# A two-layer decoder trunk in which the first feed-forward product becomes seven 2x2 block products

## The chip, the core and the metric

The kernel runs on one core of one Trainium2 chip, in one launch. The metric is the device time of a run in microseconds (us). Profiles and traces are of one execution each.

## What is computed

A decoder trunk of two layers over 1024 tokens of width 1024, all in f32. In each layer a modulation vector (`silu(c) @ W_ada + b`) gives shifts, scales and gates. A first half mixes differential attention and a gated convolution branch. The change is in the second half:

```python
x = x + (1.0 + gate1) * mixed
h2 = rms_norm(x, norm2_g[l]) * (1.0 + scale2) + shift2
f_gate, f_up = jnp.split(h2 @ w_ffn_in[l], 2, axis=-1)
x = x + (1.0 + gate2) * ((jax.nn.silu(f_gate) * f_up) @ w_ffn_out[l])
```

`w_ffn_in` is 1024 x 5632 (22 gate tiles and 22 up tiles of 128 columns), `w_ffn_out` is 2816 x 1024.

## The kernel before, in words

Activations lie transposed: 128 features on the partitions, tokens along the free axis, in two halves of 512 tokens (`HF`); `xs[j]` is feature tile j of the residual. Every f32 matrix operand is split into a high and a low float32r part, and a product is three matmuls per 128-feature tile: high x high, high x low, low x high. `wslab` (L131) loads a weight slab with a DMA on SyncE's queue (SP), rounds it to the high part on ScalarE (ACT, L139) and subtracts on GpSimd (POOL, L140) for the low part; `linear_half` (L143) then issues the three matmuls per feature tile for one token half (L148, L149, L152), each over 512 columns.

After the branch stage, the output projection runs for token half 0 and then half 1 (L745 to L757): eight output tiles of 24 matmuls (`pwo`), a residual update on VectorE (DVE, L753), squares on ACT and their sum on DVE (`sum_sq`), then `rstd_bcast` (a matmul over partitions, a power on POOL, four diagonal blocks L302, four matmuls L307) and `norm_half` (L317), which writes the split normalised activations.

In the feed-forward part, `ffn_in` (L770) makes hidden tile f: 24 matmuls for the gate tile and 24 for the up tile in each token half, a sigmoid on ACT (L784), two products on DVE that read PSUM (L785, L791), and the split of the result (ACT L792, POOL L793) in SBUF. `ffn_out` (L800) multiplies two or three hidden tiles with `w_ffn_out` and adds into `xs` (L812), so that the second product follows the first in `CHUNKS` of hidden tiles and nothing of it leaves SBUF. In layer 0, 48 modulation columns of layer 1 are made on the side (`ada_col`, L182: a load, a product on POOL at L188, a sum on ACT at L189, and one-column DVE operations at L192 to L199).

The program text is not the order of execution. The kernel is traced under a planner (`schedule_with_timeline_sim=True`, L909), which gives each engine and each DMA queue an order, with a place in the text as priority, and gives buffers out of pools; a pool that opens after another closed can use the same memory, and waits tile by tile. Engines then work through their queues in that order.

## Time and profile before

| | us |
|---|---|
| three runs, median (lowest to highest) | 3072.28 (3071.28 to 3072.49) |
| span of the profiled execution | 3069.9 |
| PE busy in it | 2876.6 (94%) |
| DVE, POOL, ACT busy | 1649.2, 1461.1, 1032.7 |

The profiled execution is 2.4 us under the median of the runs: its span goes from the first to the last instruction, and the rest of a run lies around it. Busy shares are means over stages with different limits, so the stages are read one by one.

### The profile page before, as it was taken

Reading aid. Unit: us, or ns where it says so; the run is one execution under the profiler, and the core shown is the slowest. Engines: PE = TensorE matmul, PEld = TensorE weight load, DVE = VectorE, ACT = ScalarE, POOL = GpSimd, SP = SyncE. Lnnn points to the kernel's source line nnn. Section 1 sums busy time; section 2 is a strip of 40 time slices with the busy share of each in tenths; the row PEclk is TensorE's granted clock in tenths of the full one; section 3 lists DMA queues with packets and bytes.
Section 4 is the critical chain, followed back from the end, with each engine's and each line's share of the span. In section 5 each row is a group of like instructions: output and inputs, shape, how many; then the busy total and the mean of one; then the engine's idle time right before and its main releaser. Section 6 shows DMA issues by size and latency. Waiting matters only on the chain.

```text
span 3069.9 us, 34308 instructions
## 1 busy us (share of the span) xinstructions
PE 2876.6 (94%) x13072; PEld 2366.5 (77%) x13072; DVE 1649.2 (54%) x2588; ACT 1032.7 (34%) x1820; POOL 1461.1 (48%) x974
## 2 busy tenths in 40 slices
PE   3788889999989999999999788999999999999998
PEld 3666768887768888888878677788888888888886
DVE  8899997644866211221278999774545211222126
ACT  4235445444444111111142455544534111111112
POOL 6856674435888332223342676554355232323323
PEclk9999999999989999999999999999999999999998
DMA  7611211245545111111142111222442111111113
GB/s 271 218 62 59 69 35 69 90 161 190 170 163 171 50 42 52 52 48 49 45 148 82 46 52 56 73 73 86 175 151 96 46 44 50 52 50 48 42 50 109
DMA packets 108502, 275.99 MB, mean 90 GB/s; under 512 B 10736, under 2 KB 38768, under 8 KB 108336
## 3 DMA queue, kind: packets, MB, share of 16 engines
q1 hardware_dynamic: 108336, 273.79, 25.9%
q8 instruction: 103, 1.69, 0.2%
q14 instruction: 63, 0.52, 0.1%
HBM read 235.90 MB, written 37.85 MB: 89 GB/s over the span
## 4 chain that ended last, share of the span: by engine, by line
PE 66%; DVE 24%; POOL 4%; DMA 2%; issue 2%; ACT 2%; POOLq 0%; SPq 0%; DVEq 0%; ACTq 0%
DVE uc L585 11%; PE pfg L149 5%; PE pfu L149 5%; PE pfg L152 5%; PE pfu L152 5%; PE pfg L148 5%; PE pfu L148 5%; PE pfo L148 5%; PE pfo L152 5%; PE pfo L149 5%; PE pg L152 2%; PE pg L148 2%; PE pg L149 2%; PE py L149 2%; PE py L152 2%
## 5 line engine op out<-in xcount | busy, mean ns | idle before, releaser
L140 POOL TENSOR_TENSOR wl<-wraw,wh 128x1024 fp32r<-128x1024 f32 (+2 forms) x296 | 672.5, 2274 | 1021.4 <-ACT wh L139 571.0
L139 ACT CAST wh<-wraw 128x1024 fp32r<-128x1024 f32 (+2 forms) x296 | 288.2, 974 | 732.8 <-PE pfo L149 353.2
L585 DVE SCALAR_TENSOR_TENSOR uc<-uc,vec 128x512 f32<-128x512 f32 x360 | 379.0, 1053 | 5.6
L812 DVE SCALAR_TENSOR_TENSOR x<-pfo,gcol,x 128x512 f32<-128x512 f32 x256 | 191.0, 749 | 265.0 <-PE pfo L152 264.9
L149 PE MATMUL pfg<-gl,wh 128*128 128x512 f32 x704 | 277.0, 393 | 4.7 <-DVE gl L329 3.6
L148 PE MATMUL pfo<-gh,wh 128*128 128x512 f32 x704 | 275.3, 391 | 4.1 <-DVE x L812 3.5
L148 PE MATMUL pfg<-gh,wh 128*128 128x512 f32 x704 | 276.3, 392 | 0.0
L148 PE MATMUL pfu<-gh,wh 128*128 128x512 f32 x704 | 275.3, 391 | 0.0
L149 PE MATMUL pfu<-gl,wh 128*128 128x512 f32 x704 | 275.2, 391 | 0.0
L149 PE MATMUL pfo<-gl,wh 128*128 128x512 f32 x704 | 274.8, 390 | 0.0
L149 PE MATMUL pg<-hl,wh 128*128 128x512 f32 x640 | 254.6, 400 | 14.3 <-DVE hl L511 14.3
L148 PE MATMUL pg<-hh,wh 128*128 128x512 f32 x640 | 254.0, 401 | 9.6 <-ACT hh L510 8.9
L785 DVE TENSOR_TENSOR fsg<-pfg,fsg 128x512 f32<-128x512 f32 x88 | 60.8, 691 | 375.5 <-ACT fsg L784 372.0
L791 DVE TENSOR_TENSOR fsg<-pfu,fsg 128x512 f32<-128x512 f32 x88 | 60.8, 691 | 328.0 <-PE pfu L152 327.9
L152 PE MATMUL pfo<-gh,wl 128*128 128x512 f32 x704 | 201.4, 391 | 0.0
L581 POOL TENSOR_TENSOR uc<-uc,ct 128x512 f32<-128x512 f32 x120 | 167.3, 1394 | 70.0 <-ACT ct L580 69.3
L793 POOL TENSOR_TENSOR gl<-fsg,gh 128x512 fp32r<-128x512 f32 x88 | 115.5, 1313 | 168.9 <-ACT gh L792 168.0
L152 PE MATMUL pg<-hh,wl 128*128 128x512 f32 x640 | 174.8, 403 | 0.0
L152 PE MATMUL pfu<-gh,wl 128*128 128x512 f32 x704 | 174.1, 390 | 0.0
L152 PE MATMUL pfg<-gh,wl 128*128 128x512 f32 x704 | 173.9, 390 | 0.0
L420 ACT ACTIVATE e<-psc,nb 128x512 f32<-128x512 f32 (+2 forms) x192 | 110.1, 578 | 169.1 <-DVE nb L417 148.9
L149 PEld LDWEIGHTS pfg<-gl,wh 128*128 128x128 f32 x704 | 133.4, 189 | 34.8 <-DVE gl L329 7.4
(228 smaller groups left out, 6143.1 us busy)
## 6 DMA issues: line engine op xcount, KB each, us to landing
wraw<-in_w_ffn_in_dram SPq DMA_DIRECT2D x100, 512.0 KB
adraw<-in_ada_w_dram SPq DMA_DIRECT2D x96, 512.0 KB
wraw<-in_w_in_dram SPq DMA_DIRECT2D x72, 512.0 KB
wraw<-in_w_ffn_out_dram SPq DMA_DIRECT2D x48, 384.0 KB
gd<-graw SPq DMA_DIRECT2D x64, 256.0 KB
gin<-gd SPq DMA_DIRECT2D x32, 512.0 KB
wraw<-in_w_out_dram SPq DMA_DIRECT2D x32, 512.0 KB
x<-in_xT_dram SPq DMA_DIRECT2D x16, 512.0 KB
```

Of the source, the lines that this page charges most:

```text
L139: S.copy(wh, raw)
L140: G.tensor_tensor(wl, raw, wh.bitcast(F32), op=ALU.subtract)
L148: PE.matmul(ps, wh[:, wc], rhs(0, k, hf), start=(k == 0), stop=False)
L149: PE.matmul(ps, wh[:, wc], rhs(1, k, hf), start=False, stop=False)
L152: PE.matmul(ps, wl[:, wc], rhs(0, k, hf), start=False, stop=(k == nk - 1))
L420: S.activation(e[:, n0:n1], pss[b][:, 0:n1 - n0], AF.Exp, bias=nb, scale=0.125, accum_out=sx[:, 2 * b + c:2 * b + c + 1])
L581: G.tensor_tensor(acc, acc, t, op=ALU.add)
L585: E.scalar_tensor_tensor(acc, u[:, k:k + HF], w, acc, op0=ALU.mult, op1=ALU.add)
L785: V.tensor_tensor(sgs[hf], ps, sgs[hf], op=ALU.mult)
L791: V.tensor_tensor(sgs[hf], ps, sgs[hf], op=ALU.mult)
L793: G.tensor_tensor(gl[:, hs], sgs[hf], gh[:, hs].bitcast(F32), op=ALU.subtract)
L812: V.scalar_tensor_tensor(xs[j][:, hs], ps, g2[:, j:j + 1], xs[j][:, hs], op0=ALU.mult, op1=ALU.add)
```

## The change

The first feed-forward product is done by `Group` for a pair of weight tiles (gate f, up f) as a 2x2 block product: two halves of the 1024 input features by two output tiles, times two feature halves by two token halves. Seven products `product(p)` of 12 matmuls each take the place of eight (96 matmuls). The operands of the weight side are sums made on DVE (`operand`), those of the activation side (`MV[1]` to `MV[7]`) are made once per layer, and the outputs are put together by `take1` to `take7` from PSUM. The gated product goes to a DRAM tensor `gf`; the residual after the output projection goes to `xm`. When all 22 groups are done, the second product runs by itself: for each token half, blocks of `gf` are loaded and split (`gblock`), and each of eight output tiles is one accumulation over all 22 hidden tiles, with `w_ffn_out` loaded and split once per token half. Modulation columns of layer 1 are made on DVE (`ada_col` without its last argument) beside groups 2 to 17. The convolution buffers and the rotary tables move into a pool of each layer, and the split activations are kept in units of four feature tiles. Cut to its core (comments that go, and `ffn_in` and `ffn_out`, which go whole, are left out):

```diff
-CHUNKS = [3, 3, 3, 3, 3, 3, 2, 2]
...
+    def rope_load(pl):
+        d3 = rope["d"]
+        Ct = rope["C"] = pl.tile([P, T], F32, name="Ct")
+        St = rope["S"] = pl.tile([P, T], F32, name="St")
...
+    def hunit(name, pl=None, tag="H", bufs=8):
+        return (pl or hp).tile([P, 4, HF], F32R, tag=tag, name=name, bufs=bufs)
+    class Parts:
+        def __init__(self, units):
+            self.units = units
+        def at(self, j):
+            return self.units[j // 4][:, j % 4, :]
     def hparts(name):
-        return [hp.tile([P, KT, HF], F32R, tag="H", name=f"{name}{p}", bufs=4) for p in "hl"]
+        return [Parts([hunit(f"{name}{p}{u}") for u in range(2)]) for p in "hl"]
...
+    xm = dr.tile([KT, P, T], F32, name="xm")
+    gf = dr.tile([FT, P, T], F32, name="gf")
...
+        csk = ExitStack()
+        cvp = csk.enter_context(pool("conv", side="right"))
+        rope_load(cvp)
...
+        fst = ExitStack()
+        H2 = fst.enter_context(pool("hextra"))
+        F = fst.enter_context(pool("ffn"))
+        def h2unit(name):
+            return hunit(name, H2, "H2", 6)
+        def split_into(hi, lo, src, E):
+            S.copy(hi, src)
+            E.tensor_tensor(lo, src, hi.bitcast(F32), op=ALU.subtract)
+        HS = [slice(hf * HF, hf * HF + HF) for hf in range(2)]
+        MV = {}
         for hf in range(2):
-            hs = slice(hf * HF, hf * HF + HF)
+            hs = HS[hf]
             Sq = nt("Sq")
             for j in range(KT):
                 ps = psct("pwo")
...
                 V.scalar_tensor_tensor(xs[j][:, hs], ps, gcol[l][0][:, j:j + 1], xs[j][:, hs],
                                        op0=ALU.mult, op1=ALU.add)
                 sum_sq(Sq, xs, hf, j)
+                DQ.dma_start(xm[j][:, hs], xs[j][:, hs])
             pb = rstd_bcast(Sq, 1.0 / D, 1e-6, "prn")
...
+            for q in range(2):
+                p = (1, 2, None, 3)[hf * 2 + q]
+                if p:
+                    un = h2unit if hf == 0 else hunit
+                    MV[p] = [un(f"b{p}{n}") for n in "hl"]
+                for jj in range(4):
+                    j = q * 4 + jj
+                    t = nt("ntt")
+                    V.scalar_tensor_tensor(t, xs[j][:, hs], acol[l][1][:, j:j + 1], pb, op0=ALU.mult, op1=ALU.mult)
+                    S.activation(xs[j][:, hs], t, AF.Identity, bias=modb[l][:, 24 + j:25 + j])
+                    if p:
+                        split_into(MV[p][0][:, jj, :], MV[p][1][:, jj, :], xs[j][:, hs],
+                                   V if hf and jj % 2 else G)
+        for jj in range(4):
+            a11, a12 = (xs[jj][:, h] for h in HS)
+            a21, a22 = (xs[4 + jj][:, h] for h in HS)
+            V.tensor_tensor(a11, a12, a11, op=ALU.subtract)
+            V.tensor_tensor(a12, a22, a12, op=ALU.subtract)
+            V.tensor_tensor(a22, a22, a11, op=ALU.subtract)
+        for p, x0, h in ((6, 4, 1), (7, 0, 1), (5, 0, 0), (4, 4, 0)):
+            MV[p] = [(h2unit if p == 4 else hunit)(f"b{p}{n}") for n in "hl"]
+            for jj in range(4):
+                x = xs[x0 + jj][:, HS[h]]
+                if p == 4:
+                    V.tensor_tensor(x, xs[4 + jj][:, HS[1]], x, op=ALU.subtract)
+                split_into(MV[p][0][:, jj, :], MV[p][1][:, jj, :], x, V if jj % 2 else G)
+        xpool.close()
+        R = fst.enter_context(pool("ffnr", side="right"))
         if l + 1 < L:
-            cs1 = silu_c(F, 2)
+            cs1 = silu_c(R, 2)
+        def bank(name):
+            return next(banks)(name)
+        def utile(name):
+            return F.tile([P, HF], F32, tag="u", name=name, bufs=11)
+        class Group:
+            def __init__(self, f):
+                self.f = f
+                r1 = wp.tile([P, D], F32, tag="wraw", name="wraw", bufs=2)
+                r2 = F.tile([P, D], F32, tag="fraw", name="fraw", bufs=3)
+                DQ.dma_start(r1, a["w_ffn_in"][l, f])
+                DQ.dma_start(r2, a["w_ffn_in"][l, FT + f])
+                self.a11, self.a12, self.a21, self.a22 = r1[:, 0:HF], r1[:, HF:D], r2[:, 0:HF], r2[:, HF:D]
+                self.s1 = None
+            def operand(self, p):
+                if p > 2 and self.s1 is None:
+                    s1 = self.s1 = F.tile([P, HF], F32, tag="s1", name="s1", bufs=2)
+                    V.tensor_tensor(s1, self.a21, self.a22, op=ALU.add)
+                    V.tensor_tensor(self.a21, self.a11, self.a21, op=ALU.subtract)
+                    V.tensor_tensor(self.a11, s1, self.a11, op=ALU.subtract)
+                    V.tensor_tensor(self.a12, self.a12, self.a11, op=ALU.subtract)
+                return {1: self.a11, 2: self.a12, 3: self.a12, 6: self.a11, 7: self.a21, 5: self.s1, 4: self.a22}[p]
+            def product(self, p):
+                wt = wp.tile([P, D], F32R, tag=next(wtags), name="wt", bufs=2)
+                wh, wl = wt[:, 0:HF], wt[:, HF:D]
+                split_into(wh, wl, self.operand(p), G)
+                ps = bank("pf")
+                bh, bl = MV[p]
+                for k in range(4):
+                    wc = slice(k * P, (k + 1) * P)
+                    PE.matmul(ps, wh[:, wc], bh[:, k, :], start=(k == 0), stop=False)
+                    PE.matmul(ps, wh[:, wc], bl[:, k, :], start=False, stop=False)
+                for k in range(4):
+                    PE.matmul(ps, wl[:, k * P:(k + 1) * P], bh[:, k, :], start=False, stop=(k == 3))
+                getattr(self, f"take{p}")(ps)
+            def silu(self, c):
+                sg = utile("sg")
+                S.activation(sg, c, AF.Sigmoid)
+                G.tensor_tensor(c, c, sg, op=ALU.mult)
+            def out(self, hf, c, up):
+                V.tensor_tensor(c, c, up, op=ALU.mult)
+                DQ.dma_start(gf[self.f][:, HS[hf]], c)
+            p3 = u4 = None
+            def take1(self, ps):
+                self.u2 = utile("u2")
+                S.copy(self.u2, ps)
+            def take2(self, ps):
+                self.c11 = utile("c11")
+                V.tensor_tensor(self.c11, ps, self.u2, op=ALU.add)
+                self.silu(self.c11)
+            def take3(self, ps):
+                if self.u4 is None:
+                    self.p3 = utile("p3")
+                    S.copy(self.p3, ps)
+                else:
+                    V.tensor_tensor(self.u4, ps, self.u4, op=ALU.add)
+                    self.silu(self.u4)
+            def take6(self, ps):
+                V.tensor_tensor(self.u2, ps, self.u2, op=ALU.add)
+            def take7(self, ps):
+                self.u3 = utile("u3")
+                V.tensor_tensor(self.u3, ps, self.u2, op=ALU.add)
+            def take5(self, ps):
+                self.c22 = utile("c22")
+                V.tensor_tensor(self.u2, ps, self.u2, op=ALU.add)
+                V.tensor_tensor(self.c22, ps, self.u3, op=ALU.add)
+                self.u4 = self.u2
+                if self.p3 is not None:
+                    G.tensor_tensor(self.u4, self.u4, self.p3, op=ALU.add)
+                    self.silu(self.u4)
+            def take4(self, ps):
+                V.tensor_tensor(self.u3, self.u3, ps, op=ALU.subtract)
+                self.out(0, self.c11, self.u3)
+                self.out(1, self.u4, self.c22)
+        wtags = itertools.cycle(("wh", "wl"))
+        banks = itertools.cycle((psct, p1, psct, p1, psct, p1, pmt, pmt))
+        for fs, order in [((0, 1), (1, 2, 3, 6, 7, 5, 4))] + [((f,), (1, 2, 6, 7, 5, 3, 4)) for f in range(2, FT)]:
+            gs = [Group(f) for f in fs]
+            for p in order:
+                for g in gs:
+                    g.product(p)
+            if l + 1 < L and fs[0] >= 2:
+                for t in range(3 * fs[0] - 6, min(3 * fs[0] - 3, 48)):
+                    ada_col(l + 1, t, cs1, R, 2)
+        fst.close()
+        xpool = ExitStack()
+        xp = xpool.enter_context(pool(f"y{l}", side="right"))
+        xs = [xp.tile([P, T], F32, tag=f"x{j}", name=f"x{j}") for j in range(KT)]
+        gst = ExitStack()
+        GP = gst.enter_context(pool("gbuf"))
         g2 = gcol[l][1]
...
+        NB = (FT + 3) // 4
+        def gblock(hf, b):
+            un = [hunit(f"g{n}") if b >= 4 + hf else hunit(f"g{n}", GP, "G", 10) for n in "hl"]
+            for k in range(4 * b, min(4 * b + 4, FT)):
+                t = GP.tile([P, HF], F32, tag="gs", name="gs", bufs=3)
+                DQ.dma_start(t, gf[k][:, HS[hf]])
+                split_into(un[0][:, k % 4, :], un[1][:, k % 4, :], t, V if k % 2 else G)
+            return un
+        nxt = [gblock(0, b) for b in range(NB)]
+        for j in range(KT):
+            DQ.dma_start(xs[j], xm[j])
         for hf in range(2):
...
+            hs = HS[hf]
+            gb = nxt
+            if hf == 0:
+                nxt = [gblock(1, 0)]
             Sq = nt("Sq")
-
-            def post(hf, j, Sq=Sq, hs=hs):
+            for j in range(KT):
+                ps = (psct, pmt)[j % 2]("pfo")
+                spans = [(0, 8), (8, 16), (16, FT)]
+                if hf and j == KT - 1:
+                    spans = spans[::-1]
+                for n, (k0, k1) in enumerate(spans):
+                    wh, wl = wslab(a["w_ffn_out"][l, j][:, k0 * P:k1 * P], k1 - k0)
+                    for k in range(k0, k1):
+                        wc = slice((k - k0) * P, (k - k0 + 1) * P)
+                        bh, bl = gb[k // 4]
+                        PE.matmul(ps, wh[:, wc], bh[:, k % 4, :], start=(n == 0 and k == k0), stop=False)
+                        PE.matmul(ps, wh[:, wc], bl[:, k % 4, :], start=False, stop=False)
+                        PE.matmul(ps, wl[:, wc], bh[:, k % 4, :], start=False, stop=(n == 2 and k == k1 - 1))
+                V.scalar_tensor_tensor(xs[j][:, hs], ps, g2[:, j:j + 1], xs[j][:, hs],
+                                       op0=ALU.mult, op1=ALU.add)
                 sum_sq(Sq, xs, hf, j)
                 if l + 1 < L:
                     DQ.dma_start(xd[j][:, hs], xs[j][:, hs])
-
-            for j in range(0, KT, 2):
-                ffn_out(f0, nf, j, (hf,), post)
+            if hf == 0:
+                nxt += [gblock(1, b) for b in range(1, NB)]
             pb = rstd_bcast(Sq, 1.0 / D, 1e-6, "prn")
             if l + 1 < L:
...
```

## Rows read from the trace of the kernel before

**Rows 1.** The page: span, busy times, and PE in 40 slices (tenths)

```profile
span 3069.9 us, 34308 instructions
...
PE 2876.6 (94%) x13072; PEld 2366.5 (77%) x13072; DVE 1649.2 (54%) x2588; ACT 1032.7 (34%) x1820; POOL 1461.1 (48%) x974
...
PE   3788889999989999999999788999999999999998
```

**Rows 2.** Stretches: length; PE, PEld, DVE, ACT, POOL busy; granted clock; DMA share; GB/s

```profile
0.00:40.00 40.00, 7.70 (x32) 7.05 (x32) 29.02 (x42) 16.99 (x25) 27.05 (x24) 1.00 0.81 304
733.70:837.10 103.40, 95.17 (x403) 77.56 (x402) 72.23 (x72) 45.62 (x67) 74.67 (x32) 0.95 0.56 196
837.10:886.80 49.70, 38.44 (x145) 29.22 (x144) 41.41 (x45) 22.25 (x35) 38.33 (x18) 0.83 0.44 152
1000.00:1490.00 490.00, 490.00 (x2163) 405.84 (x2163) 101.59 (x140) 84.90 (x110) 146.71 (x80) 1.00 0.15 48
2240.00:2328.30 88.30, 88.30 (x398) 73.22 (x397) 43.24 (x53) 31.79 (x41) 42.08 (x18) 1.00 0.40 143
2328.30:2360.00 31.70, 31.70 (x149) 26.50 (x148) 18.95 (x27) 13.41 (x18) 16.41 (x8) 1.00 0.26 83
```

**Rows 3.** The chain that ended last, in order of time: start, us, what

```profile
170.41 2.08 DMA cd<-uc
172.56 5.01 DMA uc<-ud
...
748.03 8.85 DMA wraw<-in_w_out_dram
...
794.92 9.36 DVE dg L302 x4
...
1547.24 4.84 DMA wraw<-in_w_ffn_in_dram
...
3018.14 5.12 DMA wraw<-in_w_ffn_in_dram
```

**Rows 4.** Groups of instructions with their shapes: xcount | busy us, mean ns

```profile
L793 POOL TENSOR_TENSOR gl<-fsg,gh 128x512 fp32r<-128x512 f32 x88 | 115.5, 1313 | 168.9 <-ACT gh L792 168.0 <-PE pfo L149 0.8
...
L139 ACT CAST wh<-wraw 128x512 fp32r<-128x512 f32 x28 | 17.4, 620 | 49.3 <-PE pfu L149 19.7 <-PE pfo L149 10.2 <-DMA wraw<-in_w_ffn_out_dram 10.1
...
L785 DVE TENSOR_TENSOR fsg<-pfg,fsg 128x512 f32<-128x512 f32 x88 | 60.8, 691 | 375.5 <-ACT fsg L784 372.0 <-POOL gl L793 3.6
...
L191 DVE SCALAR_TENSOR_TENSOR adraw<-adraw,cs 128x1024 f32<-128x1024 f32 x48 | 62.2, 1299 | 13.9 <-DMA adraw<-in_ada_w_dram 13.9
...
L511 DVE TENSOR_TENSOR hl<-ht,hh 128x512 fp32r<-128x512 f32 x16 | 11.2, 707 | 0.0
```

**Rows 5.** Instructions of DVE and POOL around 379 us: start, us, instruction

```profile
378.75 2.41 POOL L140 TENSOR_TENSOR wl<-wraw,wh 128x1024 fp32r<-128x1024 f32 x1 [0.49 <-ACT wh L139]
...
379.11 2.59 DVE L585 SCALAR_TENSOR_TENSOR uc<-uc,vec 128x512 f32<-128x512 f32 x1
...
381.11 1.54 POOL L581 TENSOR_TENSOR uc<-uc,ct 128x512 f32<-128x512 f32 x1
```

**Rows 6.** DMA issues on SP's queue, in the gates' stretch and in layer 1

```profile
559.14 0.33 SPq L645 DMA_DIRECT2D gd<-graw  x1
561.08 0.35 SPq L137 DMA_DIRECT2D wraw<-in_w_in_dram  x1
565.82 0.32 SPq L645 DMA_DIRECT2D gd<-graw  x1
...
2242.06 0.33 SPq L137 DMA_DIRECT2D wraw<-in_w_out_dram  x1
2242.45 4.29 SPq L752 DMA_DIRECT2D x<-xd  x8
```

**Rows 7.** DVE in layer 1, from the last residual update to the second norm

```profile
2328.29 0.75 DVE L753 SCALAR_TENSOR_TENSOR x<-pwo,gcol,x 128x512 f32<-128x512 f32 x1 [2.38 <-PE pwo L152]
...
2342.62 2.73 DVE L322 SCALAR_TENSOR_TENSOR ntt<-x,acol,prn 128x512 f32<-128x512 f32 x4 [1.18 <-PE prn L307]
```

More of the change, by code (lines that the diff above doesn't have):

```diff
@@ L74, in trunk @@
     hp = top.enter_context(pool("hbuf"))
-    cvp = top.enter_context(pool("conv"))
     ntp = top.enter_context(pool("ntemp"))
@@ L199, in ada_col @@
             V.tensor_scalar(gcol[l][b // 3][:, j:j + 1], m, 1.0, None, op0=ALU.add)
-    Ct = cp.tile([P, T], F32, name="Ct")
-    St = cp.tile([P, T], F32, name="St")
+    rope = {}
     def rope_tables(pl):
@@ L519, in hrhs @@
         def hrhs(part, k, hf, hh=hs_parts):
-            return hh[hf][part][:, k, :]
+            return hh[hf][part].at(k)
         def glu(c, evs=None):
@@ L674, in trunk @@
         osk.close()
+        csk.close()
         B = bst.enter_context(pool("branch"))
@@ L730, in trunk @@
                         hs = slice(hf * HF, hf * HF + HF)
-                        S.copy(mparts[hf][0][:, j, :], ta_[:, hs])
-                        V.tensor_tensor(mparts[hf][1][:, j, :], ta_[:, hs],
-                                        mparts[hf][0][:, j, :].bitcast(F32), op=ALU.subtract)
+                        S.copy(mparts[hf][0].at(j), ta_[:, hs])
+                        V.tensor_tensor(mparts[hf][1].at(j), ta_[:, hs],
+                                        mparts[hf][0].at(j).bitcast(F32), op=ALU.subtract)
         def mrhs(part, k, hf, mm=mparts):
-            return mm[hf][part][:, k, :]
+            return mm[hf][part].at(k)
         bst.close()
```

84 lines of the change are left out of this document (10 added, 74 removed).

## The prediction

> **What bounds the kernel now.** I began with the page: PE is busy 94% of the span, and its slices show 9 almost everywhere but the start and the two convolution stretches [rows 1]. A mean over stages says little, so I next read stretches. In the feed-forward part of layer 0, from 1000 to 1490 us, PE is busy for all 490.00 us over 2163 matmuls at granted clock 1.00, that is 0.2265 us for one, while DVE, ACT and POOL are busy for 102, 85 and 147 us [rows 2]: there a removed matmul is removed time. The same stage is not equally clean in both layers. The output projection takes 103.4 us in layer 0 and 88.3 in layer 1, at nearly the same matmul count, and the start of the feed-forward part needs 49.7 us for 145 matmuls in layer 0 at clock 0.83, against 31.7 us for 149 at 1.00 in layer 1 [rows 2]. The chain of waits tells why: an 8.85 us wait for a weight load, and four small diagonal operations of DVE that take 9.36 us together [rows 3], in a stretch where POOL also makes layer 1's modulation columns. Last, the queue of SP shows whether loads can run ahead of the text: weight loads go out between two stores of the gates, and eight residual loads go out together although the text has one per output tile [rows 6].
>
> **What goes.** Each of 22 hidden tiles needs 84 matmuls instead of 96, in two layers: 528 x 0.2265 = **119.6 us** off PE's path. The second product keeps its count (22 x 3 x 16 per layer).
>
> Modulation columns leave the output projection of layer 0, since their pool opens only when the first norm's sums are done. What they may give back is the difference of the layers: 103.4 - 88.3 = 15.1, and 49.7 - 145 x 31.7/149 = 18.9, together 34.0 [rows 2]. The 8.85 us load wait [rows 3] comes with eight residual loads that stay, so I take **22 us**, between 0 and 34.
>
> Near the end of each layer PE waits 4.84 and 5.12 us for slabs of the last hidden tiles [rows 3]; with uniform slabs of 8 k-tiles (24 x 0.2265 = 5.4 us of PE each) they go: **10 us**, between 0 and 10.
>
> **What is added, stage by stage.**
>
> *Groups in steady state.* PE needs 84 x 0.2265 = 19.0 us. ACT has 7 casts, 2 sigmoids and a copy, 10 x 0.62 = 6.2 us [rows 4]: beside PE. DVE has 7 operations that read PSUM, 7 x 0.69 = 4.8 us, four operand sums and two products from SBUF, 6 x 0.71 = 4.3 us [rows 4]. POOL has 7 subtractions and 2 products of 512 columns, 9 x 1.31 = 11.8 us [rows 4]. Layer 1 is therefore PE-bound (11.8 + 4.3 = 16.1 even if POOL and DVE exclude each other). They do exclude each other when DVE reads two SBUF tiles: a convolution step that began at 379.11 beside a POOL subtraction (378.75 to 381.16) took 2.59 us and ended 0.54 us after it, and POOL's next one then took 1.54 [rows 5]. In layer 0, groups 2 to 17 also carry three modulation products each on DVE, 3 x 1.30 = 3.9 us [rows 4], so the shared time is 11.8 + 4.3 + 3.9 = 20.0 us against 19.0: 1.0 us over in 16 groups, **+16 us**, between 0 and 48. The Trainium skill, GPSIMD Engine Reference, section Specifications, says that GpSimd's SBUF interfaces are shared with VectorE and contend with DVE instructions that have two SBUF inputs. By that rule the 20.0 us stand as a floor, and by PE alone it would be 19.0; the rows agree with the rule.
>
> Stores of a group (two of 256 KB) and the next group's loads go through SP; by [rows 6] the planner lets loads pass, and their wait costs nothing while two or three raw buffers are ahead. If that cover is gone, see the last rival.
>
> *Entry.* From the last residual update to the first product of the second norm layer 1 took 2342.62 - 2328.29 = 14.3 us [rows 7], with two small PE steps queued behind blocks of 24 matmuls; with blocks of 12 I take 14.3 - 2 x 2.7 = 8.9. PE has 48 matmuls that need only half 0 (products 1 and 2 of two groups), 10.9 us. Product 3 needs the fifth norm product: 8.9 + 5 x 0.68 [rows 7] + two ACT steps of 0.62 + 1.31 = 14.8, so PE waits 4 us. Its two runs last to 20.3. Product 6 needs DVE to do eight norm products (to 14.3), two subtractions and twelve sums, 14 x 0.71 = 9.9, with about two POOL operations let in between (2.6), and a last split (1.3): 28. Three of its four k-tiles are there earlier, so I count 6 of these 8 us. With a dip of the clock after the wait, as in the 0.83 of [rows 2], **12 us per layer**, between 4 (all but product 3 hidden) and 25 (the sums not begun before product 3 ends).
>
> *Reload.* A 256 KB store took 2.08 us and the load behind it 5.01 us at worst [rows 3]. With three buffers, a tile costs (2.1 to 5.0 + 0.62 + about 1.0 for a split on DVE or POOL)/3 = 1.2 to 2.2 us; PE eats one in 0.68 us. Blocks 0 and 1 take the memory of products 1 and 2, which the last group ends with 16 and 13 us to go, so 8 tiles can be ready. The other 14 need 17 to 31 us, PE needs 22 x 0.68 = 15: a wait of 4 to 18 us, **9 per layer**. If nothing runs ahead, 26 tiles, the residual and a slab are 11.5 MB, at the 304 GB/s of the first stretch [rows 2] 38 us.
>
> *Second half.* 18 tiles of half 1 come in as blocks of half 0 are done, over 15 us of the last output tile and 15 of the next: 18 x 1.2 to 2.2 = 22 to 40 against 30. **2 us per layer**, up to 17 (5.2 MB at 304 GB/s) if none is early. Slabs are split twice as often, 22 x 128 columns in 15 us of PE, POOL 7.2 us: hidden.
>
> *First half of a layer.* Pools move, the rotary tables are filled twice: 0, give or take 6 for another plan of the queues.
>
> **Sum.** -119.6 - 22 - 10 + 16 + 24 + 18 + 4 = -89.6. On the profile's 3069.9 [rows 1] that is 2980.3; the profiled execution stands 2.4 under the median, so **2983 us**. All good ends give 2920, all bad ends far over 3072.
>
> **Rivals.** *A: the shared interface sets layer 0.* The three sums ahead of product 6 each wait out a POOL operation, 3 x (0.71 + 1.31) = 6.1 instead of 2.1 us, and the four weight buffers don't absorb it: groups 2 to 17 at 23 us instead of 20, 48 us more, 3031. For it: [rows 5]. Against: three products (8 us) of lead. 0.13.
>
> *B: the reload doesn't overlap.* 38 instead of 9 and 17 instead of 2 per layer: 2983 + 58 + 30 = 3071, no change. For it: the pool of the reloaded blocks opens when the groups' pool closes. Against: pools wait tile by tile, and [rows 6]. 0.10.
>
> *C, the other side: SP keeps the order of the text.* A group's loads would stand behind the stores of the group before, which wait for its last product: two loads (1.05 MB at 304 GB/s, 3.4 us, and 2.1 more), a cast, a subtraction and the 1.3 us to the store make 8.7 us of idle PE in each of 40 groups, 348 us, 3331. It decides from 2.2 us per group on (89/40). Against: [rows 6], where loads pass stores. 0.05.
>
> *D: all waits hidden.* Entry and reload at 4 each, nothing at the halves and for the interface, all 34 back in layer 0: 2983 - 16 - 10 - 4 - 16 - 12 = 2925. 0.12.
>
> That fewer matmuls don't shorten anything would need an engine over 19 us per group; only A has one.
>
> **How the numbers follow.** The forecast (2945 to 3015) has 0.55, D 0.12, A 0.13, B 0.10 (spread over 3040 to 3080), C 0.05; 0.05 is for what I don't see. What a measurement of this kernel can tell from no change is about 0.2%, 6 us. Faster: 0.55 + 0.12 + 0.13 + 0.04 of B + 0.02 = 0.86. Slower: C, 0.03 of B, 0.02 = 0.10. Same: 0.04. The range 2932 to 3045 takes in the forecast, A and the upper part of D and leaves out B, C and the end of D.
>
> **What would show it.** 1848 matmuls of the first product per layer at 0.2265 us with PE full in layer 1; a wait of PE of about 10 us at product 6 and after the last group; slower groups in layer 0, with DVE sums stretched by POOL; the output projection of layer 0 near 88 us. I am wrong if PE is idle in each group, if waits at the two passages add up to over 40 us a layer, or if an earlier stage grows.

## The result and the profile after

The changed kernel takes **3109.70 us** (median of 4 runs, 3109.18 to 3115.12) against 3071.78 for the kernel before on the same chip (3068.62 to 3072.49): ratio **1.0127**, 95% interval 1.0113 to 1.0141. It is slower, by 38 us, where I had forecast 89 us less. The profiled execution has a span of 3113.3 us; it is the slowest of the four runs (3115.12 us), 5.4 us over their median, so the stages below add up to some 5 us more than in a median run. From the page of the changed kernel (span, busy times, PE in 40 slices):

```profile
span 3113.3 us, 35112 instructions
...
PE 2811.6 (90%) x12544; PEld 2285.4 (73%) x12544; DVE 1950.6 (63%) x2916; ACT 1151.9 (37%) x2058; POOL 1769.7 (57%) x1240
...
PE   4788889999888899979999788999997999997998
```

Beside [rows 1] the 528 matmuls are gone (13072 to 12544), but PE's busy time fell by 65 us only, since a matmul takes longer where the granted clock has fallen (50.34/160 = 0.31 us in one of the stretches below, at a mean clock of 0.78), and PE's idle time rose from 193.3 to 301.7 us. The new digits of 7 and 8 stand at the end of layer 0's output projection, in the first groups, at the entry of layer 1, and where the first product ends. To see how much each stage lost I cut each profile at the same four events on PE: first matmul of the output projection, first and last of the first product, last of the second product. All are starts, in us; as the last of the first product I took the last matmul with the low part of product 4's operand, 1.3 us before the product's real end, in every column alike:

| stage | before | after | kept memory, own buffers | all cures, ACT loads |
|---|---|---|---|---|
| layer 0 to its output projection | 733.9 | 737.5 | 737.7 | 737.5 |
| layer 0 output projection and norm | 103.0 | 99.9 | 100.9 | 93.3 |
| layer 0 groups (floor 418.6) | 751.1 with the next | 487.0 | 485.6 | 467.6 |
| layer 0 passage and second product (floor 239.2) | | 286.8 | 255.5 | 256.2 |
| layer 1 to its output projection | 651.1 | 654.4 | 649.9 | 653.8 |
| layer 1 output projection and norm | 89.0 | 100.9 | 100.4 | 93.4 |
| layer 1 groups | 724.5 with the next | 444.0 | 447.0 | 443.9 |
| layer 1 passage and second product | | 285.9 | 257.8 | 257.4 |

The floors are 1848 and 1056 matmuls at 0.2265 us. The last two columns are experiments below. The same stages in the stretches of the changed kernel (columns as in [rows 2]):

```profile
915.00:1075.00 160.00, 131.04 (x531) 99.29 (x530) 153.15 (x250) 34.02 (x63) 94.33 (x57) 0.98 0.68 235
2440.00:2720.00 280.00, 280.00 (x1237) 231.84 (x1236) 150.96 (x196) 89.96 (x149) 178.44 (x133) 1.00 0.25 85
2370.00:2420.00 50.00, 34.28 (x123) 26.05 (x122) 29.54 (x45) 23.89 (x43) 34.67 (x21) 0.80 0.22 79
1325.00:1395.00 70.00, 50.34 (x160) 34.46 (x160) 21.02 (x19) 22.71 (x35) 34.20 (x21) 0.78 0.54 171
2810.00:2880.00 70.00, 48.43 (x165) 33.40 (x164) 21.27 (x19) 23.48 (x37) 34.62 (x21) 0.85 0.53 166
1485.00:1520.00 35.00, 29.10 (x116) 22.50 (x116) 21.55 (x28) 15.28 (x22) 16.32 (x10) 0.90 0.42 137
2970.00:3000.00 30.00, 23.59 (x94) 18.03 (x93) 15.97 (x20) 9.24 (x14) 14.77 (x9) 0.89 0.58 191
```

At full rate 160 us hold 706 matmuls. The **first groups of layer 0** have 531, with DVE busy for 153 of 160 us. The groups of layer 1 are full (1237 in 280 us, clock 1.00). Its **entry** has 123 where 221 fit, 22 us lost. The two **passages** from the first to the second product have 160 and 165 where 309 fit, 33 us lost each, and the two **changes of halves** 116 of 155 and 94 of 132, 9 us each. Clocks of 0.78 to 0.90 are means of PE's granted clock, over stretches in which PE waited first.

What PE waits for in a passage, from the chain of waits of the changed kernel, layer 1 (start, us, what):

```profile
2811.78 0.69 DVE u L911
2812.47 2.43 DVE u L872
2814.90 0.61 DVE c L872
...
2815.53 2.19 DMA gf<-c
...
2817.73 0.32 SPq L940
...
2818.10 4.36 DMA gs<-gf
...
2822.47 0.63 ACT gh L773
...
2823.12 1.18 DVE gl L774
```

Nothing of the reload runs ahead: the first load of a hidden tile is issued at 2817.73, when the last store has landed, 6 us after the last matmul of the first product (2811.76), and the first cast is done at 2823.1. PE is idle for 10.7 us, and then waits for one tile after the other.

The first groups of layer 0, in the groups of instructions of the changed kernel on DVE from 915 to 1075 us:

```profile
L189 DVE SCALAR_TENSOR_TENSOR adraw<-adraw,cs 128x1024 f32<-128x1024 f32 x44 | 61.2, 1395 | 5.1 <-DMA adraw<-in_ada_w_dram 5.1
L190 DVE TENSOR_TENSOR mod<-mod,vec 128x1 f32<-128x1 f32 x45 | 24.4, 543 | 0.1
```

44 of layer 1's 48 modulation columns are made in 160 us, which is 531/84 = 6.3 groups: seven per group, not the three that the text has. The planner takes them as soon as their loads are there, and the groups' operand sums queue behind them on DVE.

### The profile page after: what moved, and what is told of

Read it like the earlier page. It is cut to its first block, busy times and chain, and to the rows that moved or that the text cites. A ratio compares the mean times of both kernels' runs of the same rounds, so it can differ in the third digit from the quotient of the medians.

```text
span 3113.3 us, 35112 instructions
## 1 busy us (share of the span) xinstructions
PE 2811.6 (90%) x12544; PEld 2285.4 (73%) x12544; DVE 1950.6 (63%) x2916; ACT 1151.9 (37%) x2058; POOL 1769.7 (57%) x1240
## 4 chain that ended last, share of the span: by engine, by line
PE 59%; DVE 26%; DMA 5%; POOL 4%; issue 3%; ACT 1%; SPq 0%; POOLq 0%; DVEq 0%; ACTq 0%
DVE uc L605 11%; PE pf L863 7%; PE pf L861 7%; PE pf L860 7%; PE pfo L965 4%; PE pfo L963 4%; PE pfo L964 4%; PE pg L146 3%; PE pg L147 3%; PE pg L150 3%; DVE adraw L189 2%; DMA gs<-gf 2%; PE py L147 2%; PE py L146 2%; PE py L150 2%
## 5 line engine op out<-in xcount | busy, mean ns | idle before, releaser
L138 POOL TENSOR_TENSOR wl<-wraw,wh 128x1024 fp32r<-128x1024 f32 (+1 forms) x216 | 515.2, 2387 | 558.6 <-ACT wh L137 398.6
L137 ACT CAST wh<-wraw 128x1024 fp32r<-128x1024 f32 (+1 forms) x216 | 219.6, 1017 | 462.2 <-PE pfo L964 288.0
L774 POOL TENSOR_TENSOR wt<-wraw,wt 128x512 fp32r<-128x512 f32 x176 | 250.4, 1426 | 185.6 <-ACT wt L773 172.7
L963 PE MATMUL pfo<-gh,wh 128*128 128x512 f32 x704 | 284.9, 405 | 26.5 <-ACT gh L773 24.1
L966 DVE SCALAR_TENSOR_TENSOR x<-pfo,gcol,x 128x512 f32<-128x512 f32 x32 | 24.0, 750 | 285.4 <-PE pfo L965 285.4
L963 PEld LDWEIGHTS pfo<-gh,wh 128*128 128x128 f32 x704 | 137.0, 195 | 62.5 <-ACT gh L773 29.8
L964 PEld LDWEIGHTS pfo<-gl,wh 128*128 128x128 f32 x704 | 136.7, 194 | 49.4 <-POOL gl L774 11.5
L965 PEld LDWEIGHTS pfo<-gh,wl 128*128 128x128 f32 x704 | 137.0, 195 | 37.2 <-POOL wl L138 9.9
L146 PEld LDWEIGHTS pg<-hh,wh 128*128 128x128 f32 x640 | 123.2, 193 | 36.7 <-ACT hh L527 9.4
L774 POOL TENSOR_TENSOR wt<-fraw,wt 128x512 fp32r<-128x512 f32 x88 | 131.6, 1495 | 14.5 <-ACT wt L773 14.5
L189 DVE SCALAR_TENSOR_TENSOR adraw<-adraw,cs 128x1024 f32<-128x1024 f32 x96 | 128.8, 1345 | 17.4 <-DMA adraw<-in_ada_w_dram 17.2
```

Source lines behind the costliest of these rows:

```text
L137: S.copy(wh, raw)
L138: G.tensor_tensor(wl, raw, wh.bitcast(F32), op=ALU.subtract)
L146: PE.matmul(ps, wh[:, wc], rhs(0, k, hf), start=(k == 0), stop=False)
L774: E.tensor_tensor(lo, src, hi.bitcast(F32), op=ALU.subtract)
L963: PE.matmul(ps, wh[:, wc], bh[:, k % 4, :], start=(n == 0 and k == k0), stop=False)
L964: PE.matmul(ps, wh[:, wc], bl[:, k % 4, :], start=False, stop=False)
```

## Experiments

Ratios are to the kernel before on the same chip; differences "to the changed kernel" are between medians, against 3109.70. The runs are from several chips, on which the kernel before took 3069.69 to 3073.36 us, so a difference of a few us between two of them says nothing.

### Is the gain of seven products there?

One product of each group multiplied a second time, so that PE has the 96 matmuls of eight products under the same staging:

```diff
-                for k in range(4):
...
+                for rpt in range(2 if p == 2 else 1):
+                    for k in range(4):
```

> Product 2 of each group is multiplied twice (the same 12 matmuls, with the same result), so that a group has the 96 matmuls of eight products and everything else stays. Theory (PE sets the groups but for the packed ones of layer 0): 59.8 us more in layer 1, and in layer 0 59.8 less the 18 us of about 6.5 groups in which PE waits anyway: 102 us more, near 3212. Rival (the groups are set by POOL and DVE): under 60 us more.

Measured: 3210.84 us, ratio 1.0449 (1.0433 to 1.0464), 101 us more than the changed kernel. The groups of layer 1 grew by 58.1 us (264 x 0.2265 = 59.8), those of layer 0 by 48.6, since some of the added matmuls fill the stalls there. So the seven products do save what was claimed: with the matmuls of eight, the new staging is 137 us slower than the kernel before on the same chip (3073.36).

### What do the modulation columns cost?

Layer 1's columns left out of the changed kernel, and of the kernel before:

```diff
-            cs1 = silu_c(R, 2)
+            for mt in [modb[l + 1]] + acol[l + 1] + gcol[l + 1]:
+                G.memset(mt, 1.0)
...
-                    ada_col(l + 1, t, cs1, R, 2)
+                    pass
```

> Leaves out layer 1's 48 modulation columns (their tiles are filled with ones), so this work stands nowhere. Theory P (packed columns): the planner has pulled seven of them into each of the groups from 915 to 1075 us, DVE is full there, and 542 matmuls take 160 us instead of 123: about 37 us go, near 3073, and the groups of layer 0 run with PE full like those of layer 1. Rival S (the Strassen sums themselves, through the interface that DVE and POOL share, hold layer 0 back): only some 10 us go, and DVE stays above 80% in these groups.

> The kernel before, leaving out layer 1's 48 modulation columns (their tiles are filled with ones): what they cost there. If my give-back of 22 us (between 0 and 34) was a cost of the columns in the kernel before: 3038 to 3057. If the slower output projection and start of the feed-forward part of layer 0 came from something else: within 6 us of 3072.

Measured: without them the changed kernel takes 3067.54 us (0.9981, 0.9968 to 0.9993), 42 less, and the groups of layer 0 take 447.0 instead of 487.0 us. The stretch that held 531 matmuls is full:

```profile
915.00:1075.00 160.00, 160.00 (x708) 132.53 (x707) 88.08 (x113) 50.89 (x84) 102.64 (x77) 1.00 0.27 89
```

The kernel before without them takes 3036.77 us (0.9890, 0.9875 to 0.9905), 33 less: its output projection of layer 0 falls from 103.0 to 89.0 us and its feed-forward part from 751.1 to 731.2, 33.9 in all. The two slow stretches of [rows 2] were the columns' price, nearly all of the 34.0 that I had read there. The change moved that price into the groups, and it grew from 33 to 42 us.

### Is it the packing, or the work?

First one landing buffer for the columns instead of two (silu_c and ada_col with 1 in place of 2):

> One landing buffer instead of two for layer 1's modulation columns, nothing else. Theory P (packing): with one buffer a column costs a load and a product in turn, 5 to 6 us, so about four columns fall to a group of 19 to 20 us and are spread over some 12 groups: at least half of the 42 us that e1 gave come back, near 3085. Rival (any column between the groups' sums costs its own time on DVE): 3105 to 3110.

Measured: 3095.96 us (1.0075, 1.0057 to 1.0094), between the two forecasts. The groups of layer 0 went to 476.4 us; the output projection of layer 1, which the edit does not touch, went from 100.9 to 93.3 by another order of the queues (why, below). Then the columns were tied to the groups:

```diff
-            cs1 = silu_c(R, 2)
+            cs1 = silu_c(R, 3)
...
                 S.copy(self.u2, ps)
+                if l + 1 < L and 2 <= self.f < 18:
+                    gate = R.tile([P, D], F32, tag="adraw", name="gate", bufs=3)
+                    S.copy(gate[:, 0:HF], ps)
...
-                    ada_col(l + 1, t, cs1, R, 2)
+                    ada_col(l + 1, t, cs1, R, 3)
```

> Layer 1's 48 modulation columns stay in the groups of layer 0, but a third landing buffer is shared with a tile that each group's first product writes, so that the columns can't run more than about one group ahead: three per group instead of about seven in each of six. Theory P (packing is what makes the groups of layer 0 slow; three columns per group cost 20.0 instead of 19.0 us as predicted): groups of layer 0 from 487 us to about 460, total 20 to 30 us under the changed kernel, some 3085. Rival S (48 columns cost DVE the same 40 us wherever they stand among groups): within 8 us of the changed kernel.

Measured: 3101.60 us (1.0102, 1.0087 to 1.0117); groups of layer 0 487.5 us, as if nothing had been done. That looks like the rival's case, but the stall is another one. With six buffers in place of three:

> As the paced run, with six landing buffers in place of three, so that a column's load can go out a group before it is needed. The paced run left the groups of layer 0 at 487.5 us, but with a new loop: the last store of a group, behind it on SP a column's load, and DVE waiting 4.1 us per group for it with the operand sums queued behind. Theory P (order, not work: three columns per group cost 1.0 us of it as predicted): groups of layer 0 at 450 to 465 us, total 3075 to 3088. Rival S (DVE and POOL together are the bound with three columns per group): groups at 475 us or more, total over 3095.

Measured: 3105.98 us (1.0109, 1.0093 to 1.0126), groups 487.5 again. The timeline of this run, first SP, then DVE (start, us, instruction), shows why:

```profile
1043.75 0.33 SPq L873 DMA_DIRECT2D gf<-u  x1
1045.46 0.33 SPq L873 DMA_DIRECT2D gf<-c  x1
1045.84 1.39 SPq L183 DMA_DIRECT2D adraw<-in_ada_w_dram  x3
...
1045.36 0.68 DVE L886 TENSOR_TENSOR c<-pf,u 128x512 f32<-128x512 f32 x1
1049.72 1.93 DVE L189 SCALAR_TENSOR_TENSOR adraw<-adraw,cs 128x1024 f32<-128x1024 f32 x1 [3.69 <-DMA adraw<-in_ada_w_dram]
1051.58 1.77 DVE L846 TENSOR_TENSOR s<-fraw 128x512 f32<-128x512 f32 x1
...
1054.41 0.15 DVE L190 TENSOR_TENSOR mod<-mod,vec 128x1 f32<-128x1 f32 x1
```

The columns' loads stand on SP behind the two stores of the group before, DVE waits 3.7 us for the first of them, and the next group's operand sum (L846) queues behind it. This is my rival C, the order of the text on SP, at a place where I had not looked. So a third version gives these loads to ACT:

```diff
-        DQ.dma_start(raw, a["ada_w"][l, t])
+        (S if l else DQ).dma_start(raw, a["ada_w"][l, t])
```

> As the paced run with six landing buffers, with the columns' loads issued by ACT instead of SP. With six buffers the groups stayed at 487.5 us and the same loop stood: a group's last store, behind it on SP a column's load, DVE waiting 4.3 us per group for it. Theory Q (SP's order: the load stands behind the store, and what waits is the operand sums behind the column in DVE's order): the wait of DVE for column loads falls below 1 us per group and the groups of layer 0 to 450 to 468 us, total 3075 to 3090. Rival S (DVE and POOL with three columns per group are the bound): groups at 475 us or more whatever issues the load, total over 3095.

Measured: 3088.80 us (1.0052, 1.0034 to 1.0070), groups of layer 0 468.1 us. One stretch with the loads on SP and the same one with them on ACT:

```profile
955.00:1235.00 280.00, 256.27 (x1082) 199.73 (x1081) 206.83 (x313) 74.90 (x139) 166.58 (x116) 1.00 0.41 147
```

```profile
955.00:1235.00 280.00, 271.35 (x1151) 212.76 (x1150) 260.91 (x334) 79.68 (x147) 197.80 (x123) 1.00 0.45 159
```

84 x 280/1151 = 20.4 us per group. Spread out and loaded in time, three columns cost a group 1.4 us over its 19.0 (21 us in 16 groups); packed they cost 2.5 (40.0/16), and late behind the stores 2.7 (84 x 280/1082 - 19.0). The rival (work alone sets the 487 us) falls; what is left of it is DVE busy for 261 of 280 us. Pacing alone gave nothing; whether the loads on ACT would do the same without the pacing was not run.

### What holds the reload back?

Three guesses: the store and the load of gf meet as one tensor (gf as 22 tensors); the landing buffers' memory comes free late (landing buffers from the general pool); the memory of the reloaded blocks comes free late, too (the pool of the half-0 operands stays open and holds the first three blocks).

```diff
-    gf = dr.tile([FT, P, T], F32, name="gf")
+    gf = [dr.tile([P, T], F32, name=f"gf{f}") for f in range(FT)]
```

> The DRAM tensor of the gated product becomes 22 tensors, one per hidden tile. Theory T (a load of any tile waits for the last store into the one tensor): the first reload goes out some 10 us before the last group ends, and the wait of about 31 us per layer at the passage falls to about 10: 40 us less, near 3070. Rival M (the buffers of the reload take memory of the groups' tiles, and that memory is released by the last store): the first reload still goes out about 6 us after the last matmul of the groups, and the time stays at 3110 within 5.

```diff
-                t = GP.tile([P, HF], F32, tag="gs", name="gs", bufs=3)
+                t = nt("gs")
```

> The reload's landing buffers are taken from the small pool that lives through the whole kernel (four buffers) instead of three in memory of the groups. Theory T (one tensor): no change in when the first reload goes out, 3110, or some 5 us less from the fourth buffer. Rival M (memory): the first reload goes out before the last group ends and 20 to 40 us go, 3070 to 3090.

```diff
-        fst = ExitStack()
-        H2 = fst.enter_context(pool("hextra"))
+        hst = ExitStack()
+        H2 = hst.enter_context(pool("hextra"))
+        fst = ExitStack()
...
-            un = [hunit(f"g{n}") if b >= 4 + hf else hunit(f"g{n}", GP, "G", 10) for n in "hl"]
+            if b >= 4 + hf:
+                un = [hunit(f"g{n}") for n in "hl"]
+            elif hf <= b < 3 + hf:
+                un = [h2unit(f"g{n}") for n in "hl"]
+            else:
+                un = [hunit(f"g{n}", GP, "G", 4) for n in "hl"]
...
-                t = GP.tile([P, HF], F32, tag="gs", name="gs", bufs=3)
+                t = nt("gs")
...
+        hst.close()
```

> The pool that holds the operands of products 1, 2 and 4 stays open into the second product, and its six units take the first three blocks of the reload; landing buffers come from the small pool, as in e3. Theory Q (memory of a pool that closes is handed on only when the planner has placed every instruction of the groups, so the reload stands behind the last store in each queue): now blocks 0 and 1 are split before the last matmul of the groups, and the passage costs PE some 10 us per layer instead of 31: 40 us less, near 3070. Rival R (the rate of the reload itself, about 1.6 us per tile against the 0.68 us that PE needs, is the cost wherever it begins): 5 to 15 us less.

Measured: 3113.49 us (1.0125, 1.0109 to 1.0141) for the first, no effect: here too the first reload goes out when the last store has landed. 3120.57 us (1.0151, 1.0134 to 1.0168) for the second: four loads do go early, but the first cast of a reloaded tile stands at 2816.6 us, 1.2 us before the end of the first product and right behind the groups' last sigmoid on ACT (2816.09), and PE then starves as before. On DVE, too, the first subtraction of the reload (2821.63) follows the groups' last product (2820.86). 3094.66 us (1.0064, 1.0043 to 1.0085) for the third: PE's first wait between the products falls from 10.7 us to none, and the stretches of the third kernel, passage and change of halves, are

```profile
2785.00:2840.00 55.00, 48.23 (x192) 36.38 (x191) 31.57 (x25) 24.51 (x39) 41.90 (x25) 0.94 0.56 181
2930.00:2980.00 50.00, 39.01 (x137) 27.69 (x136) 21.54 (x25) 17.99 (x26) 27.17 (x16) 0.85 0.55 176
```

192 of 243 matmuls, 12 us lost where it was 33, but 137 of 221 at the change of halves, 19 us where it was 9. The total, 15 us less, is the number that rival R named, but not for its reason alone: the late start was a cost of its own, and part of what it gave back was lost again at the change of halves. Both halves now share four landing buffers with the norm's temporaries. The next kernel keeps the memory as well, and gives the rest five landing buffers of its own, block 0 of half 1 other memory, and all splits of reloaded tiles to DVE:

```diff
-            if b >= 4 + hf:
+            if b >= 4 + hf or b < hf:
...
-                un = [hunit(f"g{n}", GP, "G", 4) for n in "hl"]
+                un = [hunit(f"g{n}", GP, "G", 2) for n in "hl"]
...
-                t = nt("gs")
+                t = nt("gs") if hf == 0 and b < 3 else GP.tile([P, HF], F32, tag="gs", name="gs", bufs=5)
...
-                split_into(un[0][:, k % 4, :], un[1][:, k % 4, :], t, V if k % 2 else G)
+                split_into(un[0][:, k % 4, :], un[1][:, k % 4, :], t, V)
```

> As the run that kept the memory of the half-0 operands for the first three reloaded blocks, but with five landing buffers of its own for everything after them, block 0 of half 1 in other memory, and all splits of reloaded tiles on DVE. That run won 22 us at the two passages and lost 10 at the change of halves. Theory B (landing buffers and POOL's splits set the rate of the reload): passage and second product at 261 to 268 us per layer (floor 239.2, changed kernel 286), total 3070 to 3080. Rival D (DRAM round trip and SP's order set it): no better than 3090.

Measured: **3055.61 us** (0.9958, 0.9941 to 0.9974), 54 less than the changed kernel, better than theory B's 3070 to 3080, and faster than the kernel before. Passage and second product take 255.5 and 257.8 us. The casts of the reloaded tiles, in the groups of the kernel with early landing buffers alone and of this one (count, min/median/max ns, first and last start), start 17 us before the end of the first product (2778.3) instead of 1.2 us before it (2817.8 in the first of the two):

```profile
L773 ACT CAST gh<-gs x8: 604/617/621, 2816.6 to 2830.1; 128x512 fp32r<-128x512 f32 x8
```

```profile
L774 ACT CAST gh<-gs x26: 608/617/626, 2761.1 to 2806.5; 128x512 fp32r<-128x512 f32 x26
...
2760.00:2820.00 60.00, 51.50 (x208) 40.53 (x207) 30.57 (x38) 25.29 (x40) 23.35 (x13) 0.94 0.59 193
2890.00:2930.00 40.00, 38.25 (x175) 31.07 (x174) 22.56 (x30) 18.50 (x27) 16.93 (x8) 1.00 0.55 172
```

The change of halves now has 175 of 177 matmuls. The three added edits were made together; which of them took passage and second product from 281.2 and 276.1 us to these values is open. Open is also why memory of the groups comes free so late: a wait for the very tile that lies there, or a planner that hands on a closed pool only behind the groups' last instructions. In the kernel with early landing buffers alone, the reload's steps follow those instructions on ACT and DVE without a gap, which speaks for the order of the queues but does not settle it.

### Why did the output projections not get faster?

The timeline of the changed kernel in layer 1, DVE, POOL, SP:

```profile
2339.33 10.39 DVE L294 TENSOR_TENSOR Sq<-Sq,sqt 128x512 f32<-128x512 f32 x2 [1.14 <-ACT sqt L293]
...
2338.53 2.57 POOL L774 TENSOR_TENSOR b2l<-x,b2h 128x512 fp32r<-128x512 f32 x2
2341.06 2.40 POOL L138 TENSOR_TENSOR wl<-wraw,wh 128x1024 fp32r<-128x1024 f32 x1
2343.42 2.59 POOL L774 TENSOR_TENSOR b2l<-x,b2h 128x512 fp32r<-128x512 f32 x2
2345.95 2.42 POOL L138 TENSOR_TENSOR wl<-wraw,wh 128x1024 fp32r<-128x1024 f32 x1
...
2338.22 12.51 SPq L789 DMA_DIRECT2D xm<-x  x2
2350.83 0.37 SPq L135 DMA_DIRECT2D wraw<-in_w_out_dram  x1
```

POOL makes low parts of weight slabs and of the operands of products 1 and 2 without a gap until 2348.4, and the first of the two sums of squares on DVE, which begins at 2339.33, lasts 9.59 us, until 0.55 us after POOL's last subtraction; the second takes 0.69. The next residual update stands behind it, on SP the store of that residual waits for it, and the weight load stands behind the store. Layer 0 has the same (9.60 us for one sum). Two cures, one for each end of this chain: low parts by DVE and POOL in turn, and stores issued by ACT.

```diff
-                                   V if hf and jj % 2 else G)
+                                   V if jj % 2 else G)
```

> At the entry, the low parts of the operands of products 1 and 2 are made by DVE and POOL in turn instead of POOL alone. Theory B (a run of subtractions on POOL without a gap shuts out a DVE sum of two SBUF tiles: 9.6 us for one sum of squares at 2339 us, behind which the residual update, its store and the next weight load wait): the stop of PE at 2351 to 2356 us goes, 5 to 8 us per layer, near 3097. Rival (the projection's stops come from DMA alone): 3110 within 4.

```diff
-                DQ.dma_start(xm[j][:, hs], xs[j][:, hs])
+                S.dma_start(xm[j][:, hs], xs[j][:, hs])
```

> The stores of the residual go out on ACT's queue instead of SP's. Theory W (a store that waits for DVE on SP holds up the weight load behind it): the output projection of layer 1 falls from 100.9 us toward 92, 5 to 9 us per layer, near 3096. Rival (the projection is slowed by the eight residual loads and by DVE, not by the order of SP's queue): 3110 within 4, or more, since ACT's own work now waits behind the stores.

Measured: 3095.05 us (1.0070, 1.0053 to 1.0087) and 3095.58 (1.0070, 1.0055 to 1.0085). The projections of layers 0 and 1 take 93.4 and 93.4 us in the first, 92.2 and 93.8 in the second, against 99.9 and 100.9. With the stores on ACT the long sum is still there, and harms nothing; DVE's timeline in that run:

```profile
2326.59 10.33 DVE L294 TENSOR_TENSOR Sq<-Sq,sqt 128x512 f32<-128x512 f32 x2 [1.14 <-ACT sqt L293]
```

So SP's queue is the link that costs. The one-buffer run, the first paced run and the one with the columns' loads on ACT got 93.3 in layer 1 without either edit: there no sum took over 2.5 us, and SP was held for 5.8 us where it had been 12.5. A difference of 7 us in one layer's projection is thus no proof by itself; the pair of both layers is, for in layer 0 only the kernels with one of the two edits are under 99.

### All cures together

The kernel with kept memory, both cures of the projections, and the columns made in the second product of layer 0, three per output tile:

> The kernel of the run before, and besides: the modulation columns made in the second product of layer 0, three per output tile, instead of in the groups; low parts of products 1 and 2's operands split by DVE and POOL in turn; stores of the modulated residual issued by ACT. Theory (the losses are separate and add up): -42 for the columns, -35 for the reload, -12 for the output projections: about 3020, 1.5% under the kernel before, with the groups of layer 0 at 444 to 448 us. Rival: DVE, which now splits the reloaded tiles and makes the columns, stretches the second product of layer 0 by 15 us or more: 3040 to 3060.

Measured: 3024.36 us (0.9851, 0.9837 to 0.9866). Groups of layer 0 443.9 us, but its second product 283.9 instead of 255.5: the rival's half came true as well. The columns, three per output tile in the text, were all made between 1294 and 1473 us, in the first two thirds of the stage. Where most was lost (first row), and as long after the stage's start in the last kernel below, which has no columns there (second):

```profile
1380.00:1480.00 100.00, 83.32 (x343) 64.11 (x343) 87.38 (x133) 33.04 (x46) 38.82 (x17) 0.97 0.71 242
1403.00:1503.00 100.00, 99.07 (x444) 81.66 (x443) 46.05 (x51) 38.00 (x52) 44.87 (x21) 1.00 0.47 148
```

343 of 441 matmuls, 22 of the 28 us, with DVE busy for 87 of 100 us and the DMA share at 0.71; which of the two holds PE back was not isolated. The same kernel with paced columns in the groups, loaded by SP and by ACT:

> The combined kernel with the columns in the groups of layer 0, paced with six buffers, in place of the second product of layer 0, where they cost 28 us. Theory P: groups of layer 0 at 450 to 465, second product of layer 0 back at 256: 3024 + 6 to 21 - 28, about 3002 to 3017. Rival S: groups at 475 or more: 3027 or more, no better than the combined kernel.

> The combined kernel with paced columns in the groups, their loads issued by ACT. Theory Q: 3024 - 28 + 6 to 24, 3002 to 3020, the fastest so far. Rival S: 3027 or more.

Measured: 3040.43 us (0.9897, 0.9882 to 0.9912), rival S with groups of layer 0 at 487 us again, and **3021.15 us** (0.9830, 0.9812 to 0.9848), 1 us over theory Q's 3002 to 3020. The last is the fastest, by little over the one with the columns in the second product: 1.7% under the kernel before, with groups of 467.6 and 443.9 us and passages of 256.2 and 257.4. From its page:

```profile
span 3019.8 us, 35018 instructions
...
PE 2785.7 (92%) x12544; PEld 2270.2 (75%) x12544; DVE 2008.7 (67%) x2968; ACT 1151.1 (38%) x2074; POOL 1717.9 (57%) x1188
```

## Why the prediction was wrong, by its steps

Predicted for the profiled execution 2980.3 us, measured 3113.3: 133.0 over (126.7 between the medians). By the cuts of the first table, with the forecast's terms put into their stages (the 22 us of give-back as 9.8 in the projection and 12.2 behind it, in proportion to 15.1 and 18.9, the late slabs as 5 per layer, passage and second product as floor and 11 us, and the groups as what is left of the stage before), the misses are: passage and second product +36.6 and +35.7, groups +24.1 and +11.5, output projections +6.7 and +11.9, first halves of the layers +3.6 and +3.3, tail -0.4. They sum to 133.0. Two of the signs of being wrong that I had named came: waits at the two passages of over 40 us a layer, and an earlier stage that grew.

- **The 528 matmuls, -119.6: right.** The groups of layer 1 run full, and 528 matmuls put back cost 101 us.
- **Reload, +9 per layer, and second half, +2: failed, the largest miss (72 us).** The step was "Blocks 0 and 1 take the memory of products 1 and 2 ..., so 8 tiles can be ready". None was: the first load goes out when the last result tile's store has landed, and passage and second product lose 47.6 and 46.7 us over the floor where I had 11. Kept memory alone, with shared landing buffers, still lost 42.0 and 36.9; with five landing buffers and DVE's splits besides, the reload starts 17 us early and 255.5 - 239.2 = 16.3 and 18.6 us are lost. So the price of 11 was too low even for a layout that this kernel does not have. It had a slip, too: 17 to 31 us less PE's 15 is a wait of 2 to 16, not of 4 to 18; the 9 is the middle of the former. Rival B named the mechanism ("the pool of the reloaded blocks opens when the groups' pool closes"), its 55 us per layer are near what was measured, and I gave it 0.10 on the strength of "pools wait tile by tile". Whether the planner does so here no run separates.
- **Groups of layer 0, +16: premise wrong.** "Groups 2 to 17 also carry three modulation products each": they came at seven per group. The columns cost 40.0 us in the groups, packed. At three per group, with loads in time, a group takes 20.4 us, where I had 20.0; that the sum of POOL's and DVE's times sets it is not isolated. The Trainium skill, GPSIMD Engine Reference, Specifications, says that GpSimd's interfaces to SBUF, shared with VectorE, contend with DVE instructions that have two SBUF inputs. The rows agree: the sum of squares of 9.59 us ends 0.55 us after POOL does.
- **Modulation out of the projection of layer 0, -22: failed.** The price was there, and larger: 33 us in the kernel before. I had held back 12 for the eight residual loads, but these stay in the kernel before without columns, and its projection falls to 89.0 us all the same. The gain in the projection was 3.1 us where I had counted 9.8. The stage got work of its own that I had costed at nothing: eight POOL subtractions and the residual's stores on SP. It is 99.9 us in layer 0, and 100.9 in layer 1 where it had been 89.0. I had counted the stores among a group's transfers, but not those of the residual ahead of weight loads.
- **Entry, +12: mis-sized**, 22 us in layer 1, inside its bounds of 4 to 25. I had let POOL in twice between the sums ahead of product 6; instead DVE's sums and splits followed one another without a gap from 2392.5 to 2404.6 us, and one POOL subtraction (1.3 us when alone) was held until they ended:

```profile
2396.92 8.86 POOL L774 TENSOR_TENSOR b6l<-x,b6h 128x512 fp32r<-128x512 f32 x1 [4.89 <-ACT b6h L773]
```

- **Change of halves, +2: mis-sized**, 9 us, inside its bound of 17.
- **First halves, 0 within 6: right**, +3.6 and +3.3. **Late slabs, -10:** the groups of layer 1 show no such wait, but nothing isolates the term.
- **The range** treated the rivals as exclusive. A and B together are 2983 + 88 + 48 = 3119 by my own prices. That this is near the measured time is in part luck: B happened, but the 40 us in the groups of layer 0 came from packed columns and not from A's three sums per group, and the projections' loss was in no rival. Rival C, which I priced for group loads only, decided in two other places, both on SP: weight loads behind residual stores, and, once the columns were paced, column loads behind result stores.

## What to carry to other kernels

When a stage is split in two through DRAM, ask which memory each tile of the second part takes and when the first part gives it free: here memory kept apart, with landing buffers and splits to match, turned 38 us of loss into 14 of gain. Work put "three per group" into the text is only a due time for a planner: twice the columns came in a bunch. Where such work shares an engine with the stage's critical sums, tie it to the groups, and issue its loads where no late store stands ahead of them. In this kernel stores on the queue that carries the loads held these up when their producer was late; issuing one of the two from ACT, or a producer that is not late, cured it.

## What the runs showed of the hardware that I had not expected

Beside a POOL subtraction, a DVE instruction with two SBUF inputs can be held far longer than that one subtraction. In [rows 5] the held step waited out one and went ahead of the next; here one sum of squares, 0.69 us when alone, took 9.59 us while POOL ran six subtractions without a gap. It goes the other way, too: the POOL subtraction of 8.86 us at the entry of layer 1 lasted while DVE ran its sums without a gap.

Size does not help. The addition of one modulation column (L190, 128x1) took 0.543 us on average among the packed columns. In the paced run with loads on ACT, all 48 in the groups of layer 0 are of two kinds: the 32 that began while POOL was idle took 0.14 to 0.15 us, the 16 that began during a POOL subtraction 1.23 to 1.24, until that subtraction ended. Two of them, from DVE's timeline:

```profile
1003.61 1.23 DVE L190 TENSOR_TENSOR mod<-mod,vec 128x1 f32<-128x1 f32 x1
1007.09 0.15 DVE L190 TENSOR_TENSOR mod<-mod,vec 128x1 f32<-128x1 f32 x1
```

What decides whether DVE goes ahead of the next POOL instruction stays open.
